# Attention scores of a hybrid decoder step: both products of a score over 128 rows

## The chip, the cores and the metric

One core of a Trainium2 chip. The metric is the device time of one execution in microseconds; the time before is the median of three runs.

## What is computed

One step of a decoder layer with 1024 prompt tokens and 8 samples: an input projection, four retention heads, four differential-attention heads, an output projection, and a gated MLP, with norms between. The change lies in the scores of the differential attention over the prompt. A head has two query and key maps of 64 features each, and for each block of 128 queries the reference forms

```python
s = jnp.einsum('bqhmd,bkhmd->bhmqk', q, dk).astype(jnp.float32) * (DH_DIFF ** -0.5)
s = s + alibi_bias(qpos, kpos, slopes)[None, :, None]
a = diff_combine(jax.nn.softmax(s, axis=-1), lam)
```

so h counts 4 heads, m counts 2 maps, and the softmax weights of the second map are subtracted, scaled, from those of the first.

## The kernel before

TensorE multiplies in a reduced float32 format (F32R), so that a float32 operand is split into a high part (rounded) and a low part (the rest), and a product becomes two or three products of parts that accumulate in one PSUM bank. The input projection does three per tile (lines 112 to 114): 128 rows, 128 columns of weights, 344 tokens.

`diff_head` (line 309) is one head of the prompt's attention. Its queries `zq`, keys `zk` and values `zv` have the features on the partitions: map 0 on partitions 0 to 63, map 1 on 64 to 127. Lines 319 to 322 split them: ScalarE rounds into `qs[0]` and `ks[0]`, VectorE subtracts to get the low parts `ql` and `kl`. Six copies within SBUF on the SP queue (lines 323 to 328), each of 64 partitions by 1024 elements, then stack the operands: afterwards `qs[m]` holds the query's high part and its low part, on 64 partitions each, and `ks[m]` holds the key's high part twice. Line 327 overwrites a half of `ks[0]` which lines 323 and 324 read, so it waits for these two.

`score` (line 337) is one tile of scores: up to 512 keys by 128 queries, for one map. It issues two matmuls that accumulate in one bank of the tag "S" (three banks):

```python
nc.tensor.matmul(sps, lhsT=qs[m][:, q], rhs=ks[m][:, n0:n1], start=True, stop=False)
nc.tensor.matmul(sps, lhsT=qs[m][r, q], rhs=kl[r, n0:n1], start=False, stop=True)
```

The first (line 342) runs over all 128 rows: high and low query by high key. The second (line 343) runs over the 64 rows `r` of its map alone: high query by low key. VectorE then adds the bias, takes the minimum and writes the tile to `pt` (line 345). For query block i the causal width is 128(i+1), so a head has 24 tiles: 12 of 512 columns and 4 each of 384, 256 and 128. The exponential (ScalarE, line 397), the combination of the maps (VectorE, lines 402 to 406), the transposes (`tr`, line 349, with TensorE's line 291) and the products with the values (`av_mm`, line 357, with TensorE's line 363) follow, two blocks later.

What lies beside it: the heads are generators whose stages are woven between the units of the input projection (lines 745 to 776), 1.42 stages for each unit of 24 matmuls. From the block e = 19 on, the samples' paged attention is woven in too: pages of keys come over the SP queue (line 459, four buffers), GpSimd multiplies them by the query (line 490) and VectorE sums them (line 481). The order on each engine is settled ahead of time by the framework's planner, by priority and its own estimate of when operands are ready; so the order in the trace differs a little from the program's. Each queue then runs strictly in that order. The projection's weights (line 97) also come over the SP queue.

Buffers: tag "aux" has eight slots of 1032 elements a partition, shared by the bias, `ql` and the `pt` tiles of a head. `zT` has eight slots for the projection's outputs. `ks0`, `ks1`, `qs0`, `qs1` and `kl` have one each.

Of the kernel before, what the change touches and what calls it, by code (L numbers as in the profile page):

```python
# [9 lines left out]
F32 = mybir.dt.float32  # L10
F32R = mybir.dt.float32r
I32 = mybir.dt.int32
AF = mybir.ActivationFunctionType
ALU = mybir.AluOpType
# [4 lines left out]
P = 128  # L19
D = 1024  # L20
T = 1024
# [14 lines left out]

# columns of the constant block
C_ID, C_ONE, C_KD, C_EV, C_OD, C_M8, C_SEL, C_M2, C_NH = 0, 128, 256, 260, 261, 262, 270, 302, 430
# [13 lines left out]
def step_kernel(ctx: ExitStack, tc: tile.TileContext, gam, g128, xT, w_in, w_o, w_f, w_y, norms, ngb, cst, subln,  # L52
                lams, rdec, alibi, alibi_s, kpool, vpool, ptab, sret, cw, cb, sconv,
                yT, yN, rsp, rss, kT, vT, cvp, cvs):
    nc = tc.nc
# [33 lines left out]

    # ---------------------------------------------------------------- helpers  # L90
    warm = cp.tile([P, 1], F32, name="warm")
# [25 lines left out]
    def rstd_1(pl, acc):  # L117
        """acc [128, n]: per-partition partial sums of squares -> diagonals of rsqrt(mean + eps), split."""
        n = acc.shape[1]
        blks = col_blocks(n)  # L120
        nb = len(blks)
        n1 = bank("t", "n1")[:, 0:nb]
        nc.vector.memset(n1[:, nb - 1:nb], 0.0)
        for b, (c, w) in enumerate(blks):
            nc.tensor.matmul(n1[0:w, b:b + 1], lhsT=acc[:, c:c + w], rhs=ones[:, 0:1], start=True, stop=True)
        ms = pl.tile([P, nb], F32, tag="ms", bufs=2, name="ms")
        nc.vector.tensor_scalar(ms, n1, 1.0 / D, EPS, ALU.mult, ALU.add)
        rr = pl.tile([P, nb], F32, tag="rr", bufs=2, name="rr")
        nc.gpsimd.tensor_tensor(rr, ms, nh[:, 0:nb], ALU.pow)
        rs = pl.tile([P, 2, nb], F32R, tag="rs", bufs=2, name="rs")  # L130
        nc.vector.tensor_copy(rs[:, 0, :], rr)
        nc.vector.tensor_tensor(rs[:, 1, :], rr, rs[:, 0, :].bitcast(F32), ALU.subtract)
        dg = pl.tile([P, 2, n], F32R, tag="dg", bufs=1, name="dg")
        for b, (c, w) in enumerate(blks):
            for i in range(2):
                nc.vector.tensor_scalar(dg[:, i, c:c + w], ident[:, 0:w], rs[:, i, b:b + 1].bitcast(F32), None,
                                        ALU.mult)
        return dg
# [21 lines left out]

    # ================================================================ phase A
    pa_cm, pa = opened("pa")
# [4 lines left out]

    # ---- load x, fold in the pre-norm gain, split
    rbc = pa.tile([P, TT], F32, name="rbc")
# [58 lines left out]

    # the first two blocks go segment by segment, as x comes in
    w2 = [split_w(raw0, parts=2)]  # L230
# [26 lines left out]
    def tail_a():  # L257
        nonlocal pb, pd, pk, msd, nlam, lcol, gs
        pb_cm, pb = opened("pb")
        pd_cm, pd = opened("pd")  # L260
        LATE["pk"], pk = opened("pk", "right")
        LATE.update(pb=pb_cm, pd=pd_cm)
        msd = pb.tile([P, 4, NS], F32, name="msd")
        # lambda, sub-norm gain
        lam_t = aux([P, 4, 64], name="lam_t")
        nc.scalar.dma_start(lam_t, lams)
        lsc = aux([P, 64], name="lsc")
        ld = pa.tile([P, 2], F32, name="ld")
        for i in range(2):
            nc.vector.tensor_tensor_reduce(lsc, lam_t[:, 2 * i, :], lam_t[:, 2 * i + 1, :], 1.0, 0.0,  # L270
                                           ALU.mult, ALU.add, ld[:, i:i + 1])
        le = pa.tile([P, 2], F32, name="le")
        nc.scalar.activation(le, ld, AF.Exp)
        nlam = pa.tile([P, 1], F32, name="nlam")
        nc.vector.scalar_tensor_tensor(nlam, le[:, 1:2], LAM0, le[:, 0:1], ALU.subtract, ALU.subtract)
        lcol = pa.tile([P, 1], F32, name="lcol")
        nc.vector.scalar_tensor_tensor(lcol, ct[:, C_OD:C_OD + 1], nlam, ct[:, C_EV:C_EV + 1],
                                       ALU.mult, ALU.add)
        gs = pa.tile([P, 1], F32, name="gs")
        nc.scalar.dma_start(gs, subln)  # L280
        nc.vector.tensor_scalar(gs, gs, 1.0 - LAM0, None, ALU.mult)
# [15 lines left out]
    def sub_norm(on, n):  # L297
        """on [128, n, 128] *= rsqrt(mean over the last axis + eps), in place."""
        ss = pa.tile([P, n], F32, tag="ss", bufs=2, name="ss")
# [7 lines left out]

    # ---- differential attention over the prompt, one head, in stages
    def diff_head(h):
        zq, zk, zv = Z.pop(16 + h), Z.pop(20 + h), Z.pop(24 + h)  # L310
        bias = aux([P, 1024], name="bias")
        nc.sync.dma_start(bias, alibi[h])
        # scores: [q_hi; q_lo] against [k_hi; k_hi], then q_hi against k_lo
        lo_h, hi_h = slice(0, 64), slice(64, 128)
        ks = [pd.tile([P, 1024], F32R, name=f"ks{m}", tag=f"ks{m}") for m in range(2)]
        qs = [pd.tile([P, 1024], F32R, name=f"qs{m}", tag=f"qs{m}") for m in range(2)]
        kl = pd.tile([P, 1024], F32R, name="kl", tag="kl")
        ql = aux([P, 1024], name="ql", dt=F32R)
        nc.scalar.activation(qs[0], zq[:, 0:T], AF.Copy)
        nc.scalar.activation(ks[0], zk[:, 0:T], AF.Copy)  # L320
        nc.vector.tensor_tensor(ql, zq[:, 0:T], qs[0].bitcast(F32), ALU.subtract)
        nc.vector.tensor_tensor(kl, zk[:, 0:T], ks[0].bitcast(F32), ALU.subtract)
        nc.sync.dma_start(ks[1][lo_h].bitcast(F32), ks[0][hi_h].bitcast(F32))
# [3 lines left out]
        nc.sync.dma_start(ks[0][hi_h].bitcast(F32), ks[0][lo_h].bitcast(F32))  # L327
        nc.sync.dma_start(qs[0][hi_h].bitcast(F32), ql[lo_h].bitcast(F32))
        vn = zv[:, 0:T].rearrange("p (a b) -> p a b", b=P)
        for g in range(2):  # L330
# [6 lines left out]
        def score(i, m, n0, w, pt, mn):  # L337
            r = slice(64 * m, 64 * m + 64)
            n1 = min(w, n0 + 512)
            sps = bank("S", "sps")[:, 0:n1 - n0]  # L340
            q = slice(i * P, (i + 1) * P)
            nc.tensor.matmul(sps, lhsT=qs[m][:, q], rhs=ks[m][:, n0:n1], start=True, stop=False)
            nc.tensor.matmul(sps, lhsT=qs[m][r, q], rhs=kl[r, n0:n1], start=False, stop=True)  # L343
            mo = pa.tile([P, 1], F32, tag="mn", bufs=6, name="mn")
# [82 lines left out]

    # ---- paged differential attention of the samples, in stages of a page
    def sample_attention():
        ptt = pk.tile([1, NS * NPAGE], I32, name="ptt")  # L430
        nc.sync.dma_start(ptt, ptab)
        # queries as rows, one sample's row on every partition
        q_ps = bank("t", "q_ps")
# [99 lines left out]
        yield  # L533
        # weights with the keys on partitions: [key, page, sample, head]
        tps = bank("t", "tps")[:, 0:256]
# [62 lines left out]

    # ---- retention, one head, in stages
    def ret_head(h):  # L600
# [8 lines left out]
        for g in range(2):  # L609
            aps = bank4("S", "aps")  # L610
            for i in range(4):
# [3 lines left out]
                                    ALU.mult)  # L615
        # natural values and keys, and the decayed queries, take the places of the transposed ones
        for g in range(2):
# [20 lines left out]
        nc.scalar.dma_start(rsp[h], st[:, 7, :])  # L638
        # samples: the state's part, sample b in row 32 * (b % 4) + b // 4
        qs, ks, vs = zs[:, h, :], zs[:, 4 + h, :], zs[:, 8 + h, :]  # L640
# [9 lines left out]
        nc.scalar.activation(sb, sb_ps, AF.Copy)  # L650
        # the new key's part
        sm8 = pr_tile([P, 4, NS], "sm8", tag="sm8", bufs=1)
# [4 lines left out]
        nc.tensor.matmul(tb[:, 8:16], lhsT=ones, rhs=sm8[:, 1, :], start=True, stop=True)  # L657
        # new keys and values as rows, in three groups of 32: hi, lo, hi against hi, hi, lo
        for j, e in enumerate((4 + h, 8 + h)):
# [57 lines left out]

    # ---- the rest of the input projection, with the heads' stages woven in
    def sides():
# [68 lines left out]

    # what is left of the sides, beside the first output blocks' products with the finished heads
    first = {}  # L790
# [28 lines left out]

    # ================================================================ phase W: output projection, both norms  # L820
    wo_cm, wo = opened("wo")
# [4 lines left out]
    def norms_stage(s, acc, mix):  # L826
        """post-norm and residual, pre-norm of the MLP, split: after segment s of the output projection."""
        yield
# [71 lines left out]

    # ================================================================ phase F: gated MLP, first product
    cwt = ft.tile([P, NF, 3], F32, name="cwt")
# [38 lines left out]
    def ffn_samples():  # L941
        '''The samples' gate rows come after the cached ones.'''
        sc1 = ft.tile([P, NF, NS], F32, name="sc1")
# [46 lines left out]

    # ================================================================ phase Y: second product, norm, residual
    # two parts with the features on partitions, then 256 columns with the tokens on partitions
    py_cm, py = opened("py", "right")
# [95 lines left out]

    # tokens on partitions  # L1090
    gb = py.tile([P, D], F32, name="gb")
# [161 lines left out]
```

## Time and profile before

| what | us |
|---|---|
| median of 3 runs (lowest, highest) | 1429.28 (1427.55, 1432.52) |
| the profiled execution's span, first to last instruction | 1426.5 |
| TensorE busy in it | 1382.5 (97%) |
| VectorE, ScalarE, GpSimd busy | 814.3, 512.1, 321.8 |

The span leaves out what lies ahead of the first and behind the last instruction; the profile gives no other time for this execution, and the median of the runs stands 2.8 us above the span. A matmul's end is modelled and overlaps the next one's start, so what a matmul costs is read from the distance between two starts, not from its own duration.

### The profile page before, as it was taken

How to read it: one execution, taken by the hardware profiler on the slowest of the kernel's cores; microseconds unless marked ns; L12 is line 12 of the kernel's file. 1: busy time of each engine (PE TensorE's matmuls, PEld its weight loads, DVE VectorE, ACT ScalarE, POOL GpSimd, SP SyncE). 2: the span in 40 equal slices, each digit the busy share in tenths (PEclk: the TensorE clock that was granted, in tenths of full speed). 3: DMA queues.
4: the chain of work that ended last, by engine and by line, in shares of the span. 5: the costliest groups of instructions: out<-in, count | busy, mean ns of one | idle time of the engine just before them, and what ended most of it. 6: DMA issues, size and time to landing. Idle time of an engine off the chain costs nothing.

```text
span 1426.5 us, 22325 instructions
## 1 busy us (share of the span) xinstructions
PE 1382.5 (97%) x8475; PEld 1315.5 (92%) x8475; DVE 814.3 (57%) x1656; ACT 512.1 (36%) x1016; POOL 321.8 (23%) x289
## 2 busy tenths in 40 slices
PE   6999989999999999999999999999999999989998
PEld 6979788888999999999999999999999999989976
DVE  7664677887589866477533323333232445575585
ACT  6243433426221225344322222222221235445544
POOL 4200084754355621332000000000000000050140
PEclk9999999999999999999999999999999999999999
DMA  5414166673355534132111101011110144344363
GB/s 214 120 48 118 41 191 198 218 212 118 132 175 177 165 129 150 60 140 110 68 52 37 60 31 60 33 57 45 45 60 30 60 169 145 121 156 141 119 201 124
DMA packets 67148, 161.59 MB, mean 113 GB/s; under 512 B 8283, under 2 KB 20699, under 8 KB 66659
## 3 DMA queue, kind: packets, MB, share of 16 engines
q1 hardware_dynamic: 60322, 148.57, 31.7%
q10 hardware_dynamic: 6720, 11.62, 2.2%
q8 instruction: 66, 1.08, 0.3%
q14 instruction: 40, 0.32, 0.1%
HBM read 134.93 MB, written 18.94 MB: 108 GB/s over the span
## 4 chain that ended last, share of the span: by engine, by line
PE 78%; DVE 9%; POOL 4%; issue 3%; DMA 3%; ACT 1%; SPq 0%; POOLq 0%; DVEq 0%; ACTq 0%
PE gp L112 6%; PE gp L113 6%; PE gp L114 6%; PE up L114 6%; PE up L113 6%; PE up L112 6%; PE ps_in L112 5%; PE ps_in L114 5%; PE ps_in L113 5%; PE ps_y L1063 4%; PE ps_y L1064 4%; PE ps_y L1062 4%; PE sps L343 2%; DVE acc_v L583 2%; PE ops L363 2%
## 5 line engine op out<-in xcount | busy, mean ns | idle before, releaser
L112 PE MATMUL ps_in<-xh,wh 128*128 128x344 f32 x672 | 227.0, 338 | 6.8 <-ACT xh L191 5.8
L113 PE MATMUL ps_in<-xl,wh 128*128 128x344 f32 x672 | 220.6, 328 | 2.3 <-DVE xl L192 2.3
L114 PE MATMUL ps_in<-xh,wl 128*128 128x344 f32 x672 | 221.2, 329 | 1.1 <-DVE wl L107 1.1
L112 PE MATMUL gp<-hh,wh 128*128 128x346 f32 x528 | 170.3, 322 | 0.0
L113 PE MATMUL gp<-hl,wh 128*128 128x346 f32 x528 | 170.0, 322 | 0.0
L114 PE MATMUL gp<-hh,wl 128*128 128x346 f32 x528 | 169.4, 321 | 0.0
L114 PE MATMUL up<-hh,wl 128*128 128x344 f32 x528 | 169.3, 321 | 0.0
L113 PE MATMUL up<-hl,wh 128*128 128x344 f32 x528 | 169.1, 320 | 0.0
L112 PE MATMUL up<-hh,wh 128*128 128x344 f32 x528 | 169.0, 320 | 0.0
L107 DVE TENSOR_TENSOR wl<-wraw,wh 128x1024 fp32r<-128x1024 f32 (+1 forms) x81 | 102.1, 1262 | 95.2 <-ACT wh L106 92.8
L106 ACT ACTIVATE wh<-wraw 128x1024 fp32r<-128x1024 f32 (+1 forms) x81 | 84.6, 1045 | 184.3 <-PE gp L113 92.0
L112 PEld LDWEIGHTS ps_in<-xh,wh 128*128 128x128 f32 x672 | 130.7, 194 | 12.8 <-ACT xh L191 5.8
L113 PEld LDWEIGHTS ps_in<-xl,wh 128*128 128x128 f32 x672 | 130.9, 195 | 4.1 <-DVE xl L192 3.7
L1013 DVE TENSOR_TENSOR wyl<-wyraw,wyh 128x1024 fp32r<-128x1024 f32 x66 | 83.5, 1265 | 87.8 <-ACT wyh L1012 86.5
L114 PEld LDWEIGHTS ps_in<-xh,wl 128*128 128x128 f32 x672 | 130.6, 194 | 2.0 <-DVE wl L107 1.4
L1062 PE MATMUL ps_y<-ah,wyh 128*128 128x388 f32 x352 | 120.4, 343 | 3.1 <-ACT wyh L1012 3.1
L1064 PE MATMUL ps_y<-ah,wyl 128*128 128x388 f32 x352 | 120.6, 343 | 0.2 <-DVE wyl L1013 0.2
L1063 PE MATMUL ps_y<-al,wyh 128*128 128x388 f32 x352 | 120.4, 342 | 0.4 <-DVE al L1024 0.4
L927 DVE SCALAR_TENSOR_TENSOR c<-gp,cwt,c 128x344 f32<-128x344 f32 (+1 forms) x66 | 37.7, 570 | 131.2 <-ACT c L925 131.2
L159 POOL TENSOR_TENSOR acc<-acc,sq 128x344 f32<-128x344 f32 (+1 forms) x56 | 58.4, 1043 | 226.4 <-ACT sq L158 160.6
L954 POOL COPY sct<-sct 128x176 f32<-128x176 f32 x1 | 0.5, 516 | 463.5 <-DVE sc L949 463.5
L925 ACT ACTIVATE c<-gp,cbt,cwt 128x344 f32<-128x344 f32 (+1 forms) x66 | 41.7, 632 | 175.3 <-PE gp L114 175.3
(251 smaller groups left out, 3008.5 us busy)
## 6 DMA issues: line engine op xcount, KB each, us to landing
wyraw<-in_w_y SPq DMA_DIRECT2D x66, 512.0 KB, 3.3
wraw<-in_w_f SPq DMA_DIRECT2D x44, 512.0 KB, 3.2
pg<-in_kpool SPq DMA_DIRECT2D x64, 256.0 KB, 3.1
pg<-in_vpool SPq DMA_DIRECT2D x64, 256.0 KB, 3.0
wraw<-in_w_in SPq DMA_DIRECT2D x27, 512.0 KB, 4.0
x<-in_xT SPq DMA_DIRECT2D x3, 1376.0 KB, 5.7
x1d<-x ACTq DMA_DIRECT2D x3, 1376.0 KB, 5.7
wraw<-in_w_o SPq DMA_DIRECT2D x8, 512.0 KB, 3.2
```

Source lines behind the costliest of these rows:

```text
L106: nc.scalar.activation(hi[:, k], raw[:, k], AF.Copy)
L107: nc.vector.tensor_tensor(lo[:, k], raw[:, k], hi[:, k].bitcast(F32), ALU.subtract)
L112: nc.tensor.matmul(ps, lhsT=wh[:, k, :], rhs=ah[:, k, n0:n1], start=(first and i == 0), stop=False)
L113: nc.tensor.matmul(ps, lhsT=wh[:, k, :], rhs=al[:, k, n0:n1], start=False, stop=False)
L114: nc.tensor.matmul(ps, lhsT=wl[:, k, :], rhs=ah[:, k, n0:n1], start=False, stop=(last and i == len(order) - 1))
L159: eng.tensor_tensor(acc, acc, sq, ALU.add)
L925: nc.scalar.activation(c[:, 0:n], gp[:, 2:2 + n], AF.Identity, bias=cbt[:, j:j + 1], scale=cwt[:, j, 2:3])
L927: nc.vector.scalar_tensor_tensor(c[:, 0:n], gp[:, 1:1 + n], cwt[:, j, 1:2], c[:, 0:n], ALU.mult, ALU.add)
L1013: nc.vector.tensor_tensor(wl, raw, wh.bitcast(F32), ALU.subtract)
L1062: nc.tensor.matmul(pss[d], lhsT=wh[:, i, w], rhs=ah, start=(f == 0), stop=False)
L1063: nc.tensor.matmul(pss[d], lhsT=wh[:, i, w], rhs=al, start=False, stop=False)
L1064: nc.tensor.matmul(pss[d], lhsT=wl[:, i, w], rhs=ah, start=False, stop=(f == NF - 1))
```

## The change

The low keys are doubled in the way the high keys already are. `kl` becomes a pair: `kl[1]`, a tile of the "aux" tag, gets map 1's low keys on both halves, and `kl[0]` gets map 0's on both halves in place; three more copies on the SP queue do it. The second matmul then runs over all 128 rows, with the same weights `qs[m]` as the first, and so also adds low query by low key. `ql` no longer takes an "aux" slot, but is written over `zq`. The rest of the diff is comments.

```diff
...
-        kl = pd.tile([P, 1024], F32R, name="kl", tag="kl")
-        ql = aux([P, 1024], name="ql", dt=F32R)
+        kl = [pd.tile([P, 1024], F32R, name="kl0", tag="kl"), aux([P, 1024], name="kl1", dt=F32R)]
+        ql = zq[:, 0:T].bitcast(F32R)
         nc.scalar.activation(qs[0], zq[:, 0:T], AF.Copy)
         nc.scalar.activation(ks[0], zk[:, 0:T], AF.Copy)
         nc.vector.tensor_tensor(ql, zq[:, 0:T], qs[0].bitcast(F32), ALU.subtract)
-        nc.vector.tensor_tensor(kl, zk[:, 0:T], ks[0].bitcast(F32), ALU.subtract)
+        nc.vector.tensor_tensor(kl[0], zk[:, 0:T], ks[0].bitcast(F32), ALU.subtract)
...
         nc.sync.dma_start(ks[0][hi_h].bitcast(F32), ks[0][lo_h].bitcast(F32))
         nc.sync.dma_start(qs[0][hi_h].bitcast(F32), ql[lo_h].bitcast(F32))
+        nc.sync.dma_start(kl[1][lo_h].bitcast(F32), kl[0][hi_h].bitcast(F32))
+        nc.sync.dma_start(kl[1][hi_h].bitcast(F32), kl[0][hi_h].bitcast(F32))
+        nc.sync.dma_start(kl[0][hi_h].bitcast(F32), kl[0][lo_h].bitcast(F32))
...
         def score(i, m, n0, w, pt, mn):
-            r = slice(64 * m, 64 * m + 64)
             n1 = min(w, n0 + 512)
             sps = bank("S", "sps")[:, 0:n1 - n0]
             q = slice(i * P, (i + 1) * P)
             nc.tensor.matmul(sps, lhsT=qs[m][:, q], rhs=ks[m][:, n0:n1], start=True, stop=False)
-            nc.tensor.matmul(sps, lhsT=qs[m][r, q], rhs=kl[r, n0:n1], start=False, stop=True)
+            nc.tensor.matmul(sps, lhsT=qs[m][:, q], rhs=kl[m][:, n0:n1], start=False, stop=True)
```

## Rows read from the trace of the kernel before

**Rows 1.** The page: span, and busy us (share of the span) xinstructions of each engine.

```profile
span 1426.5 us, 22325 instructions
PE 1382.5 (97%) x8475; PEld 1315.5 (92%) x8475; DVE 814.3 (57%) x1656; ACT 512.1 (36%) x1016; POOL 321.8 (23%) x289
```

**Rows 2.** Instructions of line 343: duration ns min/median/max, first and last start, forms.

```profile
L343 PE MATMUL sps<-kl,qs x96: 322/490/687, 75.4 to 356.6; 64*128 64x512 f32 x48, 64*128 64x128 f32 x16, 64*128 64x256 f32 x16, 64*128 64x384 f32 x16
```

**Rows 3.** Waits of TensorE, 60 to 360 us: total us, times, longest.

```profile
PE tp L291 <- DVE pt L406: 2.5, 2, 1.4
...
PE sps L342 <- DMA ks<-ks: 0.7, 1, 0.7
```

**Rows 4.** Timeline of TensorE, three stretches: start us, us, line, tiles, rows*columns.

```profile
252.41 0.44 PE L342 MATMUL sps<-ks,qs 128*128 128x384 f32 x1
252.78 0.44 PE L343 MATMUL sps<-kl,qs 64*128 64x384 f32 x1
253.16 0.49 PE L342 MATMUL sps<-ks,qs 128*128 128x512 f32 x1
253.58 0.50 PE L343 MATMUL sps<-kl,qs 64*128 64x512 f32 x1
254.01 1.38 PE L363 MATMUL ops<-z,pt 128*128 128x128 f32 x10
255.15 0.42 PE L342 MATMUL sps<-ks,qs 128*128 128x384 f32 x1
...
297.94 0.33 PE L342 MATMUL sps<-ks,qs 128*128 128x128 f32 x1
298.19 0.32 PE L343 MATMUL sps<-kl,qs 64*128 64x128 f32 x1
298.45 0.43 PE L112 MATMUL ps_in<-xh,wh 128*128 128x344 f32 x1
...
302.88 0.38 PE L342 MATMUL sps<-ks,qs 128*128 128x256 f32 x1
303.19 0.38 PE L343 MATMUL sps<-kl,qs 64*128 64x256 f32 x1
303.50 0.42 PE L112 MATMUL ps_in<-xh,wh 128*128 128x344 f32 x1
```

**Rows 5.** Timeline of TensorE, a score matmul followed by one of 128 rows.

```profile
82.05 0.39 PE L342 MATMUL sps<-ks,qs 128*128 128x512 f32 x1
82.28 0.27 PE L291 MATMUL tp<-ct,pt 128*128 128x128 f32 x1
```

**Rows 6.** Stretches: us, PE, PEld, DVE, ACT, POOL busy (xinstructions), PEclk, DMA share, GB/s.

```profile
60.00:180.00 120.00, 119.92 (x679) 100.38 (x677) 67.24 (x191) 51.92 (x123) 5.01 (x10) 0.99 0.29 85
...
220.00:280.00 60.00, 58.85 (x330) 49.25 (x331) 53.13 (x120) 25.15 (x59) 39.78 (x30) 0.97 0.62 205
...
300.00:360.00 60.00, 59.56 (x348) 50.33 (x348) 51.63 (x130) 29.41 (x59) 31.33 (x26) 1.00 0.47 145
```

**Rows 7.** The first of these stretches, line 343 alone: PE and PEld.

```profile
60.00:180.00 120.00, 20.49 (x47) 8.69 (x47) 0.99 0.29 85
```

**Rows 8.** VectorE by line and form, 60 to 360 us: busy, mean ns, idle before.

```profile
L345 DVE CUSTOM_DVE_ANT_0 pt<-sps,bias 128x512 f32<-128x512 f32 x40 | 27.5, 687 | 6.2 <-PE sps L343 5.6
```

**Rows 9.** A stretch of low clock, columns as in rows 6, and the one before it.

```profile
74.00:78.41 4.41, 4.41 (x20) 3.20 (x20) 2.92 (x11) 2.18 (x9) 0.00 (x0) 1.00 0.38 123
78.41:81.83 3.42, 3.42 (x11) 2.68 (x11) 1.51 (x8) 1.59 (x6) 0.00 (x0) 0.50 0.00 0
```

**Rows 10.** The third head's copies and first score: SP queue, TensorE, then landing times of two lines.

```profile
211.95 2.00 SPq L328 DMA_DIRECT2D qs<-ql  x1
...
220.01 0.30 PE L342 MATMUL sps<-ks,qs 128*128 128x128 f32 x1 [0.71 <-DMA ks<-ks]
...
DMA to landing us min/median/max: 3.3/3.4/4.1
...
DMA to landing us min/median/max: 3.9/5.2/5.7
```

## The prediction

> **What bounds the kernel now.** The page comes first [rows 1]: TensorE is busy for 97% of the span, no other engine for more than 57%. That says where to look, not that every busy microsecond is work, since matmul ends are modelled. Second, the instructions of the changed line [rows 2]: 96 matmuls of 64 rows between 75 and 357 us, 48 of 512 columns and 16 each of 384, 256 and 128. Third, what TensorE waited for in that stretch [rows 3]: the longest wait for another engine is 2.5 us in total, and a score waited once for one of the copies that stack the operands, 0.7 us. So TensorE sets the pace there, and what it does between two starts is the price.
>
> Fourth, therefore, the timeline of TensorE [rows 4], read from start to start. A 512-column pair (lines 342 and 343) begins at 253.16 and the next instruction at 254.01: 0.85 us. A 384-column pair takes 252.41 to 253.16, 0.75; a 256-column pair 302.88 to 303.50, 0.62; a 128-column pair 297.94 to 298.45, 0.51. Now the same width where the rows do not change: a 512-column score matmul of 128 rows followed by another of 128 rows takes 0.23 us [rows 5]. Ten 128-column matmuls of 128 rows take 254.01 to 255.15, 0.114 each [rows 4]. A pair thus costs nearly twice its columns, and the excess is about the same at every width: it sits at the two changes, from 128 rows to 64 and back.
>
> **A rule of the skill against the change.** By the rows a 64-row matmul among 128-row ones costs some 0.4 us instead of 0.23. The Trainium skill, "TensorE: Matmul & The Clock Gate", section "Why this matters for your kernels", says that a lone matmul with few contraction rows takes the same time as one with 128; by that alone the second product costs the same before and after and the change is worth nothing. The Trainium skill, "TensorEngine Tiling (Array Packing)", section "Key Properties", says that a change of tiling mode drains the engine; by that both changes of a pair are paid, and the trace agrees with 0.85 against twice 0.23. I go by the rows.
>
> **The change, part by part.**
>
> *The pairs.* After the change both matmuls have 128 rows. Price after: 512 columns 2 x 0.23 = 0.46, 128 columns 2 x 0.114 = 0.23; between them by a straight line, 256 columns 2 x 0.153 = 0.31 and 384 columns 2 x 0.192 = 0.38. Saved for a pair: 0.39, 0.37, 0.31, 0.28 from the widest to the narrowest. Sum: 48 x 0.39 + 16 x (0.37 + 0.31 + 0.28) = 18.7 + 15.4 = 34.1 us, 0.355 a pair. The multiplications and weight loads stay equal in number.
>
> *What of it reaches the end.* Of the 96 pairs 47 lie before 180 us [rows 7], where VectorE is busy 67 of 120 us [rows 6]; taking 47 x 0.355 = 16.7 us out leaves it 67 in 103. I count these whole. The other 49, 17.4 us, lie beside the sample pages, which VectorE sums: it is busy 53.13 of 60 us from 220 to 280 and 51.63 of 60 from 300 to 360 [rows 6]. A score tile of 512 needs 0.687 us of VectorE [rows 8] against 0.46 of TensorE after the change (0.85 before), and there are three banks for score tiles; so a run of scores will wait for VectorE where today VectorE waits for it, 5.6 us in all [rows 8]. The gain of these 49 lies between 0 (VectorE takes over at once) and 17.4 (which would use up more than the 6.9 and 8.4 us that VectorE idles in the two stretches); no row is nearer to one end than to the other, so I take the middle, 8.7 us.
>
> *The clock.* From 78.41 to 81.83 us the granted clock is 0.50, that is 1.2 GHz instead of 2.4, with TensorE shown as fully busy; in the 4.41 us before it the clock was 1.00, and TensorE had run a string of narrow score pairs there [rows 9]. Another such stretch follows the third head's first scores. At half clock 3.42 us do the work of 1.71. If the string gets shorter and denser one of the two may go: between 0 and 3.4 us, I take 1.7.
>
> *The three copies.* The next thing to be late: map 0's second matmul now needs a copy that waits for two others to land. For the third head, line 328 is issued until 213.95 [rows 10]. Two more issues of about 0.5 each bring 215.0; they land 3.4 to 5.2 later (medians of lines 327 and 328) [rows 10], at 218.4 to 220.2; the last copy, 0.5 to issue and 3.4 to land, is there at 222.3 to 224.1. The second score matmul would come at 220.2, so TensorE waits 2.1 to 3.9 us. In the other heads no score waited for a copy [rows 3]. The bound below is 0 (the planner puts projection units first), above four such waits, 15.6 us; I take 4. SP waits meanwhile with pages of keys and projection weights behind it. The pages have four buffers, the weights come two blocks ahead; a late page reaches VectorE through GpSimd, and that is in the half taken above.
>
> *At nothing.* `ql` over `zq`: same VectorE work, and the slot of `zq` comes free a copy's landing later; eight slots cover that, and if they did not, an evacuation would wait some 5 us once a head. `kl[1]` holds an "aux" slot for the whole head, where `ql` gave it back: six slots are left for score rows, of which three blocks of two are alive at once. If that is too few, the first score of a block waits for the transposes two blocks back: between 0 and the 2.5 us that such a dependency on line 406 costs now [rows 3]; zero taken.
>
> **Sum.** 16.7 + 8.7 + 1.7 - 4 = 23.1 us out of the profiled span of 1426.5: 1403.4. The median of the runs stands 2.8 us above that span, so 1406.
>
> **Rivals.**
>
> *All of it arrives.* VectorE's work fits into its gaps, both slow stretches go, copies stay hidden: 34.1 + 3.4 = 37.5 us, 1392. For it: TensorE's waits are few [rows 3]. Against: VectorE near full beside the pages [rows 6].
>
> *VectorE is the bound beside the pages.* None of the second 49 pairs counts, nor the clock: 16.7 - 4 = 12.7 us, 1417. For it: after the change the two stretches would hold 104.8 us of VectorE's work in 120 - 46 x 0.355 = 103.7 us. Against: today it has idle time there, and projection units lie between runs of scores.
>
> *No effect.* The pair's price belongs to the score itself (its accumulation, its operands), not to the rows: nothing is gained and 4 us of copies are added, 1433. The skill's first rule above would have it so. Against: rows 5 show the same kind of instruction at 0.23 where 128 rows follow.
>
> *The copies decide (slower).* The last copy of a head is late by two of the longest landings in series, 2 x 5.7 = 11.4 us [rows 10], at each of four heads, because SP's queue also carries the pages and waits inside the chain: 45.6 us against 27.1 gained, 1448. It decides from 6.8 us a head on. For it: the chain grows by one wait and page loads stand in the same queue. Against: one exposed wait of 0.7 us today, and work of the projection that can go first.
>
> **How the numbers follow.** A measurement of this kernel tells 0.3%, 4.3 us, from no change. Forecast, about 1397 to 1413: 0.60. All of it: 0.14. VectorE the bound: 0.17. Between that and no change: 0.03. No effect: 0.03. The copies: 0.03. The first three and a part of the fourth are faster by over 0.3%: 0.93; same 0.03; slower 0.04. The range reaches from the first rival to a little beyond the second, 1392 to 1421.
>
> **What would show it.** In the changed kernel's timeline a 512-column pair should take 0.46 us from start to start and a 128-column pair 0.23; line 343's successor should read 128 rows. TensorE should wait more often for VectorE's line 345 and its neighbours between 220 and 360 us, and VectorE's share there should rise above 0.9. The low-clock stretches near 78 and 222 us should be gone or fewer. The first score of the third head should wait for a copy of `kl`. The stretch behind the heads should be unchanged. I am wrong in the main step if a pair still takes 0.8 us, in the halving if the second heads lose or keep all, and in the sign only if copies hold each head by 7 us.

## The result, and the profile after

| | before | after |
|---|---|---|
| median of 4 runs, us (lowest, highest) | 1430.75 (1427.55, 1432.52) | 1411.89 (1406.66, 1412.81) |
| the profiled execution's span, us | 1426.5 | 1410.2 |

The ratio is 0.9871, with a 95% interval of 0.9851 to 0.9891: 18.9 us less. The line numbers after the copies move by two: the score's matmuls are now lines 344 and 345, VectorE's reading of a score tile line 347, the coefficient of the second map `cf` line 407, the combination line 408.

The page after, columns as in [rows 1]:

```profile
span 1410.2 us, 22347 instructions
PE 1353.4 (96%) x8475; PEld 1308.8 (93%) x8475; DVE 812.2 (58%) x1656; ACT 504.5 (36%) x1012; POOL 323.7 (23%) x289
```

TensorE runs the same 8475 matmuls; the other engines are busy for about as long as before. Now the changed matmuls, columns as in [rows 2], and three stretches of TensorE's timeline, columns as in [rows 4]:

```profile
L345 PE MATMUL sps<-kl,qs x96: 219/364/477, 76.8 to 333.3; 128*128 128x512 f32 x48, 128*128 128x128 f32 x16, 128*128 128x256 f32 x16, 128*128 128x384 f32 x16
```

```profile
83.81 0.39 PE L344 MATMUL sps<-ks,qs 128*128 128x512 f32 x1
84.04 0.39 PE L345 MATMUL sps<-kl,qs 128*128 128x512 f32 x1
84.27 0.32 PE L113 MATMUL ps_in<-xl,wh 128*128 128x344 f32 x1
...
235.02 0.45 PE L344 MATMUL sps<-ks,qs 128*128 128x384 f32 x1 [1.06 <-DVE mn L347]
...
241.28 1.06 PE L365 MATMUL ops<-z,pt 128*128 128x128 f32 x8
242.09 0.48 PE L344 MATMUL sps<-ks,qs 128*128 128x512 f32 x1
242.41 0.39 PE L345 MATMUL sps<-kl,qs 128*128 128x512 f32 x1
242.63 0.32 PE L114 MATMUL ps_in<-xh,wl 128*128 128x344 f32 x1
```

The last start comes 333.3 us into the span instead of 356.6. A 512-column pair that follows a wide matmul takes 84.27 - 83.81 = 0.46 us. One that follows 128-column matmuls takes 242.63 - 242.09 = 0.54: the first of its products starts its successor after 0.32, not 0.23 (what that means is said with the pairs of the prediction below). At 235.02 stands what the faster pairs brought: a score that waited 1.06 us until VectorE gave a bank back.

What TensorE waited for between 60 and 360 us, columns as in [rows 3]:

```profile
PE tp L291 <- DVE pt L408: 4.6, 4, 1.7
PE ops L365 <- ACT pt L356: 3.2, 2, 2.6
PE sps L344 <- DVE mn L347: 2.4, 5, 1.1
PE tp L291 <- DVE on L306: 2.3, 1, 2.3
PE sps L344 <- DMA qs<-z: 1.7, 1, 1.7
...
PE sps L344 <- DMA ks<-ks: 0.6, 1, 0.6
```

All rows of this view together come to 18.3 us, against 8.2 before. And the stretches, columns as in [rows 6]; the last three are of low clock:

```profile
60.00:180.00 120.00, 118.17 (x788) 111.62 (x787) 76.98 (x211) 56.96 (x140) 19.48 (x20) 1.00 0.41 116
220.00:280.00 60.00, 53.33 (x348) 49.38 (x346) 53.51 (x98) 22.38 (x50) 40.39 (x30) 1.00 0.68 201
300.00:360.00 60.00, 55.89 (x369) 52.18 (x370) 50.11 (x124) 26.33 (x59) 30.05 (x26) 0.97 0.49 153
205.00:250.00 45.00, 40.96 (x262) 36.72 (x261) 42.68 (x108) 23.01 (x55) 27.64 (x23) 1.00 0.65 204
184.63:188.04 3.41, 3.41 (x13) 3.41 (x14) 3.41 (x4) 1.64 (x2) 3.08 (x3) 0.50 0.89 258
280.20:283.62 3.42, 3.42 (x15) 3.42 (x14) 0.52 (x1) 0.00 (x0) 0.96 (x1) 0.50 0.86 229
341.64:345.06 3.42, 3.42 (x17) 3.42 (x16) 3.42 (x4) 0.02 (x1) 3.17 (x2) 0.50 0.83 249
```

TensorE is no longer busy throughout: it idles 6.67 of 60 us from 220 on. From 205 to 250 VectorE is at 42.68 of 45, or 95%.

**Where the time went.** Two sums over the whole trace carry the account. *Pairs* adds, for all 192 score matmuls, the distance to the next matmul's start, less what that one waited. *Waits* adds the rows of TensorE's view of waits over the span.

| kernel | pairs, us | waits, us | span, us |
|---|---|---|---|
| before | 69.3 | 37.6 | 1426.5 |
| after | 39.4 | 49.9 | 1410.2 |
| difference | -29.9 | +12.3 | -16.3 |

What is left, 16.3 against 29.9 - 12.3 = 17.6, is 1.3 us of other matmuls; the execution after the change was at half clock for 3.4 us more than the one before (30.7 against 27.3 us by the trace's clock records, without the stretch at the very end of each), which is an estimated 1.7 us. Of the 12.3 us the view puts 7.2 down to VectorE, 3.5 to ScalarE and 1.6 to copies. 10.0 of them lie between 60 and 360 us.

### The profile page after: what moved, and what is told of

Its sections match the earlier page's. It is cut to its first block, busy times and chain, and to the rows that moved or that the text cites. A ratio compares the mean times of both kernels' runs of the same rounds, so it can differ in the third digit from the quotient of the medians.

```text
span 1410.2 us, 22347 instructions
## 1 busy us (share of the span) xinstructions
PE 1353.4 (96%) x8475; PEld 1308.8 (93%) x8475; DVE 812.2 (58%) x1656; ACT 504.5 (36%) x1012; POOL 323.7 (23%) x289
## 4 chain that ended last, share of the span: by engine, by line
PE 72%; DVE 13%; DMA 5%; POOL 4%; issue 3%; ACT 1%; SPq 0%; POOLq 0%; DVEq 0%; ACTq 0%
PE gp L112 6%; PE gp L113 6%; PE up L114 6%; PE gp L114 6%; PE up L113 6%; PE up L112 6%; PE ps_in L112 4%; PE ps_in L114 4%; PE ps_in L113 4%; PE ps_y L1066 4%; PE ps_y L1065 4%; PE ps_y L1064 4%; DVE acc_v L585 2%; PE ops L365 1%; PE tp L291 1%
## 5 line engine op out<-in xcount | busy, mean ns | idle before, releaser
L929 DVE SCALAR_TENSOR_TENSOR c<-gp,cwt,c 128x344 f32<-128x344 f32 (+1 forms) x66 | 37.6, 570 | 131.2 <-ACT c L927 131.2
```

The source lines that it names most:

```text
L929: nc.vector.scalar_tensor_tensor(c[:, 0:n], gp[:, 1:1 + n], cwt[:, j, 1:2], c[:, 0:n], ALU.mult, ALU.add)
```

## The experiments

Theory: the gain is the row changes, and the 12 us given back are VectorE's, which is too slow beside the sample pages for a TensorE that asks sooner. Rivals: the doubled copies and the moved buffers cost it; TensorE's own order (stages released at a fixed pace) makes the waits.

**1. Rows or copies.** First, the kernel before with both products over 64 rows, so that a pair has no change inside it. It leaves out low query by high key.

```diff
-            nc.tensor.matmul(sps, lhsT=qs[m][:, q], rhs=ks[m][:, n0:n1], start=True, stop=False)
+            nc.tensor.matmul(sps, lhsT=qs[m][r, q], rhs=ks[m][r, n0:n1], start=True, stop=False)
```

> The kernel before, with the first product over the 64 rows of its map too, so that both products of a score have 64 rows; low query by high key is left out. If the price sits at the change of rows (my theory), the first product of a 512-column pair is followed by the second after 0.23 us instead of 0.41, and only where a score stands beside 128-row work is some 0.19 us still paid on either side; the kernel comes out a few us to 17 us faster than before. If a 64-row matmul is slow by itself, or a score is slow whatever its rows (rivals), both distances are about 0.42 and the time is that of before or longer.

A single execution gave 1423.17 us, beside a median of 1428.73 and a lowest of 1425.91 in 19 executions of before. The timeline of this kernel:

```profile
74.88 0.44 PE L342 MATMUL sps<-ks,qs 64*128 64x384 f32 x1
75.16 0.34 PE L343 MATMUL sps<-kl,qs 64*128 64x384 f32 x1
75.42 0.42 PE L112 MATMUL ps_in<-xh,wh 128*128 128x344 f32 x1
...
80.60 0.50 PE L342 MATMUL sps<-ks,qs 64*128 64x512 f32 x2
80.94 0.40 PE L343 MATMUL sps<-kl,qs 64*128 64x512 f32 x2
81.27 0.71 PE L363 MATMUL ops<-z,pt 128*128 128x128 f32 x4
```

The 0.23 that I expected between two products of the same 64 rows was wrong: it is 0.33 to 0.34 at 512 columns (and 0.28 at 384, where 128 rows take 0.17). But some rows have x2: where the two maps' tiles stand together, map 0's product (partitions 0 to 63) and map 1's (64 to 127) start 0.02 us apart and share the 0.33, so that four 512-column products take 0.67. All pairs together take 36.9 us, less than after the change, and still the span fell by only 5.4. Of the 32.4 us saved, 10.6 reappear on the 128-column matmuls beside the scores (line 363: 33.2 to 38.7 us from start to start, line 291: 31.8 to 36.9). Some 7 of these stand on the matmul just ahead of a score: ahead of a 64-row score it hands on (the next start follows its own) after 0.20 us, ahead of a 128-row one, in the kernel before, after 0.03 (medians of 43 and 39). Another 3.3 are low clock. TensorE's waits rise from 37.6 to 49.7; a further 4.3 us, to the measured 5.4, lie on other matmuls, and low clock is part of that too: this execution was at half clock for 37.5 us against 27.3 before, an estimated 5 us in all. This kernel has no copy more than before, and yet the same 12 us of waits.

The Trainium skill, "TensorE: Matmul & The Clock Gate", section "The mechanism", says that weight loads overlap matmuls under way only where the groups of rows differ. The 64-row products fit that: 0.02 us between products of different halves, 0.33 between products of the same half. The 128-row products do not: two on the same rows start 0.23 us apart after the change, though every matmul there has its weight load (8475 of each).

The counterpart keeps the change's copies and buffers, and runs the second product over 64 rows:

```diff
+            r = slice(64 * m, 64 * m + 64)
...
-            nc.tensor.matmul(sps, lhsT=qs[m][:, q], rhs=kl[m][:, n0:n1], start=False, stop=True)
+            nc.tensor.matmul(sps, lhsT=qs[m][r, q], rhs=kl[m][r, n0:n1], start=False, stop=True)
```

> The changed kernel with its three copies and its buffers, but the second product over 64 rows again, as before. If the gain comes from the rows alone and the copies cost little, a 512-column pair takes 0.84 us again and the time is that of the kernel before plus 0 to 6 us, ratio 1.000 to 1.004. If the gain came from the new order of the work or the buffers (rival), it stays below 0.995. If the copies take back much of the gain (second rival), it is 1.006 or more.

1429.83 us, ratio to before 1.0021 (1.0001 to 1.0040): the gain is gone. Its timeline has the old price, 0.32 to 0.41 and then 0.42 us:

```profile
81.76 0.40 PE L345 MATMUL sps<-ks,qs 128*128 128x512 f32 x1
82.08 0.49 PE L346 MATMUL sps<-kl,qs 64*128 64x512 f32 x1
82.50 0.43 PE L114 MATMUL ps_in<-xh,wl 128*128 128x344 f32 x1
```

Pairs 67.3 us, waits 40.7. With the last experiment this makes a square: cheap pairs without the copies give 12.1 us more waiting, the copies without cheap pairs 3.1. So the gain is the rows of the second product, the copies and buffers cost about 3 us (0 to 6 by the interval), and the waits come with the speed of the pairs.

**2. Is it VectorE's work on the pages?** Both kernels without the reduction that sums the pages on VectorE (the samples' scores are left out); shown for after:

```diff
-            nc.vector.tensor_reduce(sc[:, p, :, 2 * b:2 * b + 2], kp.rearrange("p h (m e) -> p h m e", m=2),
-                                    AX.X, ALU.add)
+            pass
```

> The kernel before without VectorE's sums over the key pages (line 481, 42.7 us of VectorE beside the second half of the scores); the samples' scores are left out with them. Serves as the base of the next run. VectorE waits for GpSimd at these sums, so TensorE's waits for VectorE should fall; 2 to 8 us below the kernel before.

> The changed kernel without VectorE's sums over the key pages, as in the run before this. If VectorE beside the pages took back the missing half of the gain (my theory), this comes out 27 to 34 us below the kernel before without the sums, against 19 us with them. If the late copies or the order of the scores took it (rivals), the distance stays at 16 to 22 us.

Before 1423.99 us (ratio 0.9966, 0.9954 to 0.9978), after 1403.50 (0.9820, 0.9801 to 0.9839). Between 60 and 345 us VectorE has 43 us less to do (64 reductions of 0.68 us), and the change is worth 20.5 us, against 18.9: in the rivals' range, not in that of my theory. From 220 to 280 us VectorE is now busy for 63% of the time (37.58 of 60 us) where it was 89%. Between 60 and 360 us the second kernel still waits, and for the same lines:

```profile
PE sps L344 <- DVE mn L347: 4.7, 3, 2.3
PE tp L291 <- DVE pt L408: 4.6, 2, 2.7
PE tp L291 <- DVE on L306: 3.9, 2, 3.1
```

Waits over the span go from 35.8 to 45.8 us. My theory that VectorE is full falls: taking 43 us off it gives back 2 of the 12. With the sums goes another way in which GpSimd could hold TensorE up: VectorE idled for GpSimd's products ahead of its sums (13.8 us from 60 to 345 us after the change, 13.1 before), and whatever stood behind a sum idled with it. That is not the main cause either.

**3. Is it GpSimd's work beside it?** As in 2, and GpSimd's product of each page with the query is removed as well (the pages are still loaded):

```diff
-                nc.gpsimd.tensor_tensor(kp, kp, qb.rearrange("p (a b) -> p a b", b=P), ALU.mult)
```

> The kernel before without GpSimd's products of the key pages and without VectorE's sums over them; the pages are still loaded. The samples' scores are left out. Base of the next run; a little below the kernel before without the sums alone (1424), 1416 to 1424 us.

> The changed kernel with the same left out. Theory now: beside the pages VectorE is slowed by GpSimd's work on them (VectorE's line 408 takes 1.6 us at 384 columns there, 0.6 elsewhere), and this, not VectorE's own sums, holds the scores up; then this is 27 to 34 us below the base. Rival: the late copies hold the first score tiles of a head back for some 8 us and bunch what follows, so that VectorE cannot keep up whatever the pages do; then the distance stays at 17 to 22 us.

Before 1414.74 us (0.9892, 0.9866 to 0.9917; a little below the 1416 to 1424 expected), after 1392.11 (0.9723, 0.9691 to 0.9756): 22.6 us between them, 23.8 by the profiled spans. The two ratios' intervals are each some 4 us to either side, so 22.6 and 18.9 are not told apart by the times, and 22.6 is short of the 27 to 34 that my theory gave. The rows say more: pairs fall as they did (69.4 to 40.1 us), but waits rise only from 31.0 to 34.7. That is the smaller because outside 60 to 360 us the waits fall by 2.2 us, for which no run gives a reason. Between 60 and 360 us they rise by 6.0, from 1.0 to 7.0, against 10.0 for the change itself; and 3.0 of the 6.0 are copies. What the change adds there in waits for VectorE and ScalarE is 8.5 us with everything in place, 9.3 without the sums, 3.1 without sums and products. The second kernel's waits from 60 to 360 us:

```profile
PE sps L344 <- DVE mn L347: 3.4, 3, 2.7
PE sps L344 <- DMA ks<-ks: 1.6, 1, 1.6
PE sps L345 <- DMA kl<-kl: 1.3, 1, 1.3
```

Nothing waits for lines 408 and 306 any more; what is left is bank and copies. What GpSimd does to VectorE is seen in two groups, 60 to 345 us (line, operation, tiles, shapes, count, busy us, mean ns, idle before), first after the change and then without the products:

```profile
L408 DVE SCALAR_TENSOR_TENSOR pt<-pt,cf 128x128 f32<-128x128 f32 (+7 forms) x32 | 31.7, 990 | 0.2
...
L407 DVE SCALAR_TENSOR_TENSOR cf<-sm,nlam,rs 128x1 f32<-128x1 f32 x32 | 13.4, 419 | 0.0
```

```profile
L408 DVE SCALAR_TENSOR_TENSOR pt<-pt,cf 128x128 f32<-128x128 f32 (+7 forms) x32 | 27.6, 862 | 0.6
...
L407 DVE SCALAR_TENSOR_TENSOR cf<-sm,nlam,rs 128x1 f32<-128x1 f32 x32 | 8.0, 249 | 0.0
```

One element a partition takes 419 ns on average beside the products and 249 without. In the timeline of VectorE after the change it can be seen at its worst:

```profile
233.19 1.16 DVE L407 SCALAR_TENSOR_TENSOR cf<-sm,nlam,rs 128x1 f32<-128x1 f32 x1
...
241.12 1.32 DVE L407 SCALAR_TENSOR_TENSOR cf<-sm,nlam,rs 128x1 f32<-128x1 f32 x1
```

The first of these stands right ahead of the score tile for whose bank TensorE waited 1.06 us until 235.02. The score tile behind the second is read 1.3 us later. (Without VectorE's sums but with GpSimd's products, as in 2, line 407 still takes 12.0 us.) The Trainium skill, "SBUF — State Buffer", section "SBUF: two separate sides", says that a VectorE instruction with two inputs in SBUF and a GpSimd instruction that reads SBUF shut each other out while one of them runs. The rows agree as far as they go: the same instruction is short without the products and up to five times as long beside them, while VectorE's copy on line 405, with one input, takes 146 ns beside them and 150 without.

**4. The late copies.** In the change the low keys are made in one subtraction and three copies, the third waiting for two. Here VectorE subtracts each half into its own tile, and two copies suffice, of which neither waits for the other:

```diff
-        nc.vector.tensor_tensor(kl[0], zk[:, 0:T], ks[0].bitcast(F32), ALU.subtract)
+        nc.vector.tensor_tensor(kl[0][lo_h], zk[lo_h, 0:T], ks[0][lo_h].bitcast(F32), ALU.subtract)
+        nc.vector.tensor_tensor(kl[1][hi_h], zk[hi_h, 0:T], ks[0][hi_h].bitcast(F32), ALU.subtract)
...
-        nc.sync.dma_start(kl[1][lo_h].bitcast(F32), kl[0][hi_h].bitcast(F32))
-        nc.sync.dma_start(kl[1][hi_h].bitcast(F32), kl[0][hi_h].bitcast(F32))
         nc.sync.dma_start(kl[0][hi_h].bitcast(F32), kl[0][lo_h].bitcast(F32))
+        nc.sync.dma_start(kl[1][lo_h].bitcast(F32), kl[1][hi_h].bitcast(F32))
```

> The changed kernel with a shorter chain: VectorE subtracts each map's half straight into its own tile (two instructions of 64 partitions instead of one of 128), and two copies, neither waiting for the other, fill the other halves, where three did, the last of them waiting. If the late copies bunch the scores (rival), 4 to 12 us below the changed kernel, 1400 to 1408. If GpSimd and VectorE beside the pages hold the scores up (theory), within 4 us of it, 1408 to 1416; the two more instructions a head cost VectorE about 1.2 us each.

1412.31 us (0.9876, 0.9855 to 0.9898): the same as the change. Its timeline at the third head's start:

```profile
203.53 0.61 PE L344 MATMUL sps<-ks,qs 128*128 128x128 f32 x3 [0.31 <-DMA ks<-ks]
...
204.93 0.39 PE L345 MATMUL sps<-kl,qs 128*128 128x128 f32 x2
```

The first scores start, then TensorE does projection units until the low keys are there; neither here nor in the change does a second product wait. The copies' chain is hidden by the order.

**5. The pace of TensorE's order.** Two tries at another order of the stages. One changes the constant `K_PACE` from 3.0 to 2.6 in the change's kernel (the pace at which the page stages are released):

```diff
-D_RATE, R_RATE, K_PACE, V_PACE = 1.42, 0.88, 3.0, 2.35
+D_RATE, R_RATE, K_PACE, V_PACE = 1.42, 0.88, 2.6, 2.35
```

> The changed kernel with the pages of keys woven in more thinly, 2.6 a unit of the projection instead of 3.0. If the pages beside the scores hold TensorE up (theory), 3 to 8 us below the changed kernel, as long as the pages of values behind them still end before the heads do; if they do not matter (rival), the same within 3 us or longer.

1417.40 us (0.9925, 0.9899 to 0.9950), worse than the change by 5.5 us by the medians and 7.7 by the ratios. Between 60 and 360 us the waits are little fewer (17.0 us against 18.3); new ones came behind the heads, at a place that had 0.9 us of them in the change. From this kernel's view of waits over the whole span:

```profile
PE tp L291 <- DVE m L697: 7.9, 3, 2.8
```

**6. A shorter chain on VectorE.** If `cf` holds up the score tiles behind it, then another form of it should help the change and do little for the kernel before. `cf` becomes an instruction that takes two scalars a partition beside its one input, and the reciprocals are written where they are read, which drops one copy a block:

```diff
-            nc.vector.tensor_tensor(on, OP.pop(g), R0[g].unsqueeze(2).broadcast_to([P, 4, P]), ALU.mult)
+            nc.vector.tensor_tensor(on, OP.pop(g), R0[g][:, :, 0:1].broadcast_to([P, 4, P]), ALU.mult)
...
-                R0[i // 4] = pa.tile([P, 4], F32, tag="r0", bufs=2, name="r0")
+                R0[i // 4] = pa.tile([P, 4, 2], F32, tag="r0", bufs=2, name="r0")
...
-            rs = pa.tile([P, 2], F32, tag="rs", bufs=4, name="rs")
+            rs = R0[i // 4][:, i % 4, :]
...
-            nc.vector.tensor_copy(R0[i // 4][:, i % 4:i % 4 + 1], rs[:, 0:1])
...
-            nc.vector.scalar_tensor_tensor(cf, sm[:, 0:1], nlam, rs[:, 1:2], ALU.mult, ALU.mult)
+            nc.vector.tensor_scalar(cf, sm[:, 0:1], nlam, rs[:, 1:2], ALU.mult, ALU.mult)
```

> The changed kernel with less of VectorE's work at the end of a query block: the small product of line 407 (13.4 us in all, up to 1.3 us for one element a partition beside the pages) reads one tensor and two scalars instead of two tensors, and the copy of line 405 (4.7 us) goes, since the reciprocals are kept where they are used. If VectorE held up by GpSimd takes back the gain (theory), line 407 falls to some 0.2 us each and the time by 3 to 8 us against the changed kernel, to 1404 to 1409. If VectorE is not what holds the scores up (rival), within 2 us of it.

> The kernel before with the same two edits. Theory: TensorE waits for VectorE little there, so only 0 to 4 us are gained against the kernel before, less than on the changed kernel. Rival: as much on both, 3 to 8 us; then the edits help VectorE in general and say nothing of the change.

On the change: 1404.65 us (1401.92 to 1405.50), ratio to before 0.9820 (0.9781 to 0.9858), the fastest kernel here that leaves nothing out. On the kernel before: 1427.16, ratio 0.9983 (0.9962 to 1.0005). The group of `cf` in the faster one, 60 to 345 us, and the head of its waits from 60 to 360:

```profile
L406 DVE TENSOR_SCALAR cf<-sm,nlam,r 128x1 f32<-128x1 f32 x32 | 8.6, 268 | 0.2
```

```profile
PE tp L291 <- DVE on L306: 4.3, 2, 2.3
PE tp L291 <- DVE pt L407: 4.1, 5, 1.9
```

`cf` takes 268 ns beside the products, nearly the 249 that the old form takes without them, and no score waits for its bank any more in this stretch. Waits over the span are 44.9 us, 5.0 fewer than after the change; on the kernel before the same edits leave them at 37.3, against 37.6. The ratio of the two ratios is 0.9948, 7 us, and their intervals overlap, so the size is not settled. By the profiles it is 6.5 us: 5.0 of waits, the rest matmuls, part of it less time at half clock (23.9 us against 30.7, an estimated 3.4 us). And only some 2 of the 5.0 lie between 60 and 360 us, where the waits for VectorE are no fewer than after the change (13.0 against 12.3): those for banks are gone, others have grown, as the first of the two above, which was 2.3. So the edits pay on the changed kernel and not on the one before, but that the length of `cf` is what TensorE had waited for is not shown by them; nor were the two edits tried apart.

**7. On top of it.** Two tries more. First, the change's three copies from ScalarE's queue, so that nothing stands behind them on SP:

```diff
-        nc.sync.dma_start(kl[1][lo_h].bitcast(F32), kl[0][hi_h].bitcast(F32))
-        nc.sync.dma_start(kl[1][hi_h].bitcast(F32), kl[0][hi_h].bitcast(F32))
-        nc.sync.dma_start(kl[0][hi_h].bitcast(F32), kl[0][lo_h].bitcast(F32))
+        nc.scalar.dma_start(kl[1][lo_h].bitcast(F32), kl[0][hi_h].bitcast(F32))
+        nc.scalar.dma_start(kl[1][hi_h].bitcast(F32), kl[0][hi_h].bitcast(F32))
+        nc.scalar.dma_start(kl[0][hi_h].bitcast(F32), kl[0][lo_h].bitcast(F32))
```

> The changed kernel with the two edits and with the three copies of the low keys issued from ScalarE's queue instead of SP's. If SP's wait for the copies costs through the pages and weights behind it, 2 to 5 us below the run with the two edits alone. If not, the same within 2 us; ScalarE's exponentials then stand behind the wait of the third copy, and it can come out up to 6 us longer.

1421.24 us (0.9948, 0.9931 to 0.9965), 17 worse than the two edits alone, more than the 6 that I allowed. Now the copies do hold TensorE; from its view of waits:

```profile
PE sps L345 <- DMA kl<-kl: 3.8, 2, 1.9
PE sps L344 <- DMA ks<-ks: 3.3, 2, 3.0
```

These 7 us are not all of the 17. The profiled spans are 12.3 us apart, and by the view of waits over the span 12.1 of that is waiting: 5.9 more for copies, 3.5 for ScalarE, 2.8 for VectorE. What the medians have beyond the profiled spans no trace explains. Second, the stages at the pace the pairs now have, fewer for each unit:

```diff
-D_RATE, R_RATE, K_PACE, V_PACE = 1.42, 0.88, 3.0, 2.35
+D_RATE, R_RATE, K_PACE, V_PACE = 1.30, 0.92, 3.0, 2.35
```

> The changed kernel with the two edits on VectorE, and the attention stages woven in more thinly, 1.30 a unit of the projection instead of 1.42 (the retention heads behind them at 0.92 instead of 0.88). If VectorE beside dense scores is what holds TensorE (theory), 2 to 6 us below the run with the two edits alone, 1399 to 1403. If the stages pushed behind cost as much at the end of the projection (rival, as with the thinner pages), the same or up to 8 us longer.

1414.35 us (0.9892, 0.9871 to 0.9913), 10 worse than the two edits alone. The waits gather at one place:

```profile
PE tp L291 <- DVE on L306: 13.6, 4, 6.4
```

Neither pace that was tried is better than the one that the kernel came with. That says nothing about paces not tried.

## Why the prediction was right, and where its steps were not

1406 was forecast, 1392 to 1421, faster at 0.93; 1411.9 was measured. Sign and range hold, and so does the main step, that the 64-row product was what a pair paid for; of the 23.1 us expected the runs show 18.9, the profiled spans 16.3. From 23.1 to 16.3, 4.2 us are missing from the pairs and an estimated 3.4 from the clock; the rest evens out within 1 us. What was said of VectorE came out in size, but not by its mechanism.

*The pairs* (34.1 us): 29.9 measured. That the 64 rows of the second product were the price is shown by the counterpart in experiment 1: with them back and the rest of the change kept, pairs take 67.3 us and the gain is gone. That the price sits at the two changes of rows, as I had it, is not shown: two products of the same 64 rows, with no change between them, still take 0.33 a step, against 0.23 for 128 rows. The term was mis-sized at 512 columns, which gave 14.2 us of the 18.7 that I summed; the other three widths gave 15.6 for 15.4 (a 128-column pair was cheaper than I had it both before and after, 0.49 and 0.22 us). Most of the shortfall is in the price before. My 0.85 [rows 4] is a pair behind another 64-row product, and there the first product takes 0.43 us; so it is with 17 of the 48. 25 others follow a 128-column matmul. Their first product takes 0.41, but 0.08 of it only makes up for that matmul, which hands on after 0.03 us instead of the usual 0.11. After the change, where no rows change, the same is seen:

```profile
84.59 0.39 PE L344 MATMUL sps<-ks,qs 128*128 128x512 f32 x1
84.82 0.27 PE L291 MATMUL tp<-ct,pt 128*128 128x128 f32 x1
84.85 0.48 PE L345 MATMUL sps<-kl,qs 128*128 128x512 f32 x1
85.16 0.32 PE L112 MATMUL ps_in<-xh,wh 128*128 128x344 f32 x1
```

Here 0.03 and 0.31 us take the place of 0.11 and 0.23: the sum is the same. So behind 128-row work a pair cost some 0.75 before (0.33 and 0.42, as from 81.76 in experiment 1), not 0.85, and the 0.54 after the change holds the same 0.08. It does not disturb the sum of the pairs, with 26 first products of 512 columns behind a 128-column matmul before and 25 after. All this is read from the starts; no run varied the neighbour alone.

*Half lost beside the pages* (8.7 us) *and the copies* (4 us): together 12.7 us, and 12.3 of waits measured. That the two sums agree is luck, since 8.7 was a middle taken for want of a row, and the split and the mechanism were others. By place it came out: from 180 to 360 us TensorE waits 8.3 us more than before; from 60 to 180 us, where I counted the gain whole, 1.7. Copies took 1.6 us more of waits than before, at the first scores of the third and fourth heads; the last copy of `kl`, which by my step would hold the third head, was never waited for after the change. VectorE did rise to 95%, but its load is not why: with 43 us of its work gone the waits stayed (experiment 2). In their place the runs show that most of these waits need GpSimd's products beside VectorE (8.5 us with both, 9.3 without VectorE's sums, 3.1 when the products go too, experiment 3). That they do it by making single results of VectorE late is argued from the instructions that lengthen beside the products; experiment 6 fits it in time but not in the rows between 60 and 360 us. How much of the 12 us is that, and how much stages that are released too close together, stays open: the differences, 4 and 7 us, are as large as the intervals.

*The clock* (1.7 us): wrong. Its step was that a shorter, denser string of scores would spare one of two low stretches. [Rows 9] is gone, but between 60 and 360 us there are three stretches at 0.50, 1.2 GHz, as there were three before (the third began at 204.71), only elsewhere: at 184.63 TensorE, VectorE and GpSimd are all busy. I moved the stretches; I did not remove any, and over the span the profiled execution had 3.4 us more of them, a loss of an estimated 1.7. Nothing here was made to test what sets them.

*At nothing* (`ql` over `zq`, the "aux" slot): no wait of the change names them, and the kernel that has all of it but the rows costs about 3 us, which holds these and the copies.

*The rivals.* "No effect" is refuted. The Trainium skill, "TensorE: Matmul & The Clock Gate", section "Why this matters for your kernels", would have had it so; for a product that stands among others the measured 0.42 against 0.23 decides against its rule here. "All of it arrives" fails mostly by the waits, and by 4.2 us of pairs. "VectorE the bound" named 1417 with nothing of the later pairs; its number is a little nearer to the median than mine (5.1 against 5.9 us), so the time alone does not decide between us, but its mechanism, VectorE's total load, is what experiment 2 speaks against. "The copies decide" needs 6.8 us a head; 1.6 came over all four.

## What to carry to other kernels

Read what an instruction costs from start to start, and with its neighbours: here a product of 64 rows made itself and the product ahead of it so slow that twice the rows took little more than half the time, and a distance between two starts could hold 0.08 us of the matmul ahead. When the bound engine gets faster, expect some of the gain back as waits on results that used to be early, and test the total load of their engine before blaming it. An order tuned for the old pace can still be the best of those tried for the new one.

## What the hardware showed that was not expected

Two 64-row products in different halves of the array start 0.02 us apart and share 0.33 us; two in the same half take 0.33 each, more than two of 128 rows (0.23). A 128-column matmul hands on after 0.03 us to a 128-row score product and after 0.20 to a 64-row one. A VectorE instruction on one element a partition took up to 1.32 us beside GpSimd's products, 249 ns on average without them, and 268 in a form that takes its operands as scalars. A three-copy chain moved from SP's queue to ScalarE's cost 17 us, though nothing had waited for it on SP.
